# A mixture-of-experts trunk in float32: more slots in the ring of streamed weights, one buffer for the gathered tokens, and a slot that is handed back earlier

## The chip, the cores and the metric

The kernel runs on one core of a Trainium2 chip. The metric is the device time of one execution in microseconds; the median of three runs is compared. Engines are called as the profile calls them: PE (TensorE, with its weight loads as PEld), DVE (VectorE), ACT (ScalarE), POOL (GpSimd) and SP (SyncE, which only issues transfers here).

## The reference

Two decoder layers work on 256 positions of width 1024. Each layer has a mixer, a layer norm, a feed-forward part and a second layer norm. The feed-forward part of the first layer is one dense SwiGLU of width 2816. That of the second layer is a mixture of eight SwiGLU experts of width 3584, of which each position uses two:

```python
def swiglu(x, w_gate, w_up, w_down):
    return (jax.nn.silu(x @ w_gate) * (x @ w_up)) @ w_down

def moe_swiglu(x, w_router, e_gate, e_up, e_down):
    t = x.reshape(B * S, D)
    logits = (t @ w_router).astype(jnp.float32)
    top_val, top_idx = lax.top_k(logits, TOP_K)
    top_w = jax.nn.softmax(top_val, axis=-1)
    gates = jnp.sum(jax.nn.one_hot(top_idx, N_EXPERTS) * top_w[..., None], axis=1)
    out = jnp.zeros_like(t)
    for e in range(N_EXPERTS):
        out = out + gates[:, e:e + 1] * swiglu(t, e_gate[e], e_up[e], e_down[e])
    return out
```

All weights are float32, and all eight experts' weights (352 MB of the 426 MB that the kernel reads) pass through the core once.

## The kernel before

**Weights.** They stream in units of 128 x 2048 values (1 MB, 8 KB in each partition). A product needs two parts of each unit that the PE can multiply at its fast float32 rate: `h`, a rounded copy that ACT makes, and `l`, the rest that DVE makes by a subtraction (`split`, L270 to L272; only the first unit of each gate product, `whole`, is multiplied raw). A unit so passes through one slot as `r` (raw), and then through two others as `h` and `l`.

**Slots.** There are `NS` = 16 slots in the pool `wt` and `NX` = 2 more in the pool `more`, which takes the place of the pool `mix` once the mixer of the second layer no longer needs that. The class `Stream` keeps the order of all units (`plan`, with a due time for each, counted in ticks) and the list `idle` of slots that may be taken, first in, first out. `load` takes one slot and issues a transfer on SP. `converting` takes two, for `h` and `l`, and puts the raw slot at the end of the list. `drop` puts the slot of an `l` back, `free` what is left of the oldest unit. A slot is put back where the code issues the last instruction that uses it; who takes it next waits on the chip for that instruction.

**Order.** `manual_schedule` leaves each engine's instructions in the order of the code. A tick is one step of a product: one matmul with `h` and one with `l`. At each tick the pending tasks step first, and then `pump` runs: it loads while the list is longer than `1 + max(0, freed + reserve - split)`, then converts the next unit if it is due within `lead` = 12 ticks and the list has at least two slots.

**Experts.** An expert has four groups of columns: 512, 1024, 1024 and 1024 (in the last expert in reverse). For each group come the gate product, the up product, and then the down product of the group before. A product of 1024 columns has four units of four ticks, one of 512 columns two. After an up product, `finish` copies it out of PSUM, and 13 ticks later `transposed` folds and transposes the group's hidden values and splits them into `ch` and `cl` (rings of four), by way of a tile `hid`. After a whole expert, `scatter` adds its output rows to `acc`.

**Tokens.** An expert works on the tokens that were routed to it. `gather` picks them on the PE with a one-hot matrix: the transposes L1012, a copy `pt` by ACT, two times 16 matmuls L1000, and their split into `xh` and `xl` by `parts`; `xw` is a raw copy of the first half for the unsplit units. With at most 64 tokens (`few`) the parts `h` and `l` of the tokens lie side by side in one 128 wide operand, so that two passes do; with more (`many`, a wide expert) it takes three passes. Tokens have two buffers in turn (`xh`, `xl` in the pool `act`, rings of two): the gather for expert e + 1 is started after the third group's down product of expert e and runs four ticks later, in the fourth group's gate product.

**The lines of the steps below.** `h` is L271, `l` is L272, and L1050 is a pass over an unsplit unit. L1053 and L1060 are passes of gate and up products, L1137 and L1144 those of down products, L1032 the last passes of a pair of units. L1075 and L1085 are the copies out of a gate and an up product, L1108 the fold, and L1110 to L1113 the hidden values; L991, L992 and L1025 write the gathered tokens.

Of the kernel before, what the change touches and what calls it, by code (L numbers as in the profile page):

```python
# [8 lines left out]
F32 = mybir.dt.float32  # L9
# [18 lines left out]
TAU = 16.0  # L28

NS = 16  # L30
NX = 2
NR = 6
NQ = 3
NC = 5
# [5 lines left out]
def trunk(ctx: ExitStack, tc: tile.TileContext, x, w_in, gm_ws, gm_bs, gm_ln_g, gm_ln_b, gla_wa2, gla_ba,  # L40
# [24 lines left out]
        return mix.tile(list(shape), F32, tag="m2", name=name, bufs=5)  # L65

    def tiny(name, n, dt=F32):
        return act.tile([P, n], dt, tag="tiny", name=name, bufs=10, padded_shape=[P, 32])

    def psy(name, shape=(P, 512), dt=F32):  # L70
        return ps_y.tile(list(shape), dt, tag="y", name=name)
# [220 lines left out]
    def norm(y, st, gt, bt, nm):  # L292
# [5 lines left out]
        for hf in range(2):  # L298
            s = slice(hf * 512, hf * 512 + 512)
            nc.vector.scalar_tensor_tensor(y[:, s], y[:, s], mv[:, 0:1], gt[hf], op0=ALU.subtract, op1=ALU.mult)  # L300
            nc.vector.scalar_tensor_tensor(y[:, s], y[:, s], rs, bt[hf], op0=ALU.mult, op1=ALU.add)

    def to_T(tb, nm, xT):

        xh = act.tile([P, KT, P], F32R, tag="xh", name=f"xh{nm}{tb}")
        xl = act.tile([P, KT, P], F32R, tag="xl", name=f"xl{nm}{tb}")
        xT[tb] = xh, xl
        for hf in range(2):
            tp = psw(f"tp{nm}{tb}{hf}", (P, 4, P))
            for j in range(4):  # L310
                c = (hf * 4 + j) * P
                nc.tensor.transpose(tp[:, j, :], xf[tb][:, c:c + P], ident)
            split(xh[:, hf * 4:hf * 4 + 4, :], xl[:, hf * 4:hf * 4 + 4, :], tp)
            if hf == 0:
                yield 1
# [62 lines left out]
    def transposed_parts(sg, nm, kt):  # L378

        tp = psw(f"th{nm}", (P, 4, P))  # L380
        for j in range(kt):
            nc.tensor.transpose(tp[:, j, :], sg[:, j * P:(j + 1) * P], ident)
        ch = act.tile([P, 4, P], F32R, tag="ch", name=f"ch{nm}", bufs=4)
        cl = act.tile([P, 4, P], F32R, tag="cl", name=f"cl{nm}", bufs=4)
        split(ch[:, 0:kt, :], cl[:, 0:kt, :], tp[:, 0:kt, :])
        return ch, cl

# [84 lines left out]
    def mixer(l, xT, small, ready, nxT):  # L472
# [207 lines left out]
        products([("gv", l), ("gu", l)], xT, 512, f"gm{l}", gated)  # L680
        W.lead = 12
        products([("og", l)], xT, 512, f"og{l}", out_gate)
        if l == DEPTH - 1:

            mix_only.close()
            more = ctx.enter_context(tc.tile_pool(name="more", bufs=1))
            room.extend([more] * NX)
            idle.extend(range(NS, NS + NX))
        gb = load_gb(ln_mix_g[l], ln_mix_b[l], f"mix{l}")
        py = [[psy(f"wo{l}{tb}{hf}") for hf in range(2)] for tb in range(2)]  # L690

# [134 lines left out]

    def moe(xT, ready, consts):
        iota, pri, ones, ecst, pair, fold, powers = consts
        lg = const.tile([P, 2, NE], F32, name="lg")
        plt = psy("plt", (P, 2, NE))  # L830

# [29 lines left out]
        cnt_i = const.tile([P, 1], I32, name="cnt_i")  # L861
        mask_i = const.tile([P, 1], I32, name="mask_i")
        small = const.tile([P, NE], F32, name="small")
        acc = [room[-1].tile([P, D], F32, name=f"acc{tb}") for tb in range(2)]

        def routing():
            yield 2
# [83 lines left out]
        class Expert:  # L951
# [21 lines left out]

            def one_hot(self):
                nm = self.nm
                self.oh = act.tile([P, 2, P], F32, tag="oh", name=f"oh{nm}", bufs=1)
                self.twice = self.oh
                for tb in range(2):
                    nc.vector.tensor_scalar(self.oh[:, tb, :], iota, self.rank(tb), None, op0=ALU.is_equal)
                if self.fewer is not None:  # L980
                    self.twice = s2(f"oh2{nm}", F32, (P, 2, P))
                    slot = s2(f"slot{nm}")[:, 0:P]
                    nc.vector.tensor_scalar(slot, iota, HALF - 0.5, self.fewer, op0=ALU.is_ge, op1=ALU.mult)
                    nc.vector.tensor_tensor(slot, slot, iota, op=ALU.add)
                    for tb in range(2):
                        nc.vector.tensor_scalar(self.twice[:, tb, :], slot, self.rank(tb), None, op0=ALU.is_equal)
# [21 lines left out]
            def gather(self):  # L1008
                nm = self.nm
                tp = pst(f"oht{nm}", (P, 2, P))  # L1010
                for tb in range(2):
                    nc.tensor.transpose(tp[:, tb, :], self.twice[:, tb, :], ident)  # L1012
                self.pt = act.tile([P, 2, P], F32R, tag="pt", name=f"pt{nm}")
                nc.scalar.activation(self.pt, tp, AF.Copy)
                xh = act.tile([P, KT, P], F32R, tag="xh", name=f"exh{nm}")
                xl = act.tile([P, KT, P], F32R, tag="xl", name=f"exl{nm}")
                self.x = xh, xl
                for hf in range(2):
                    p = pst(f"gx{nm}{hf}", (P, 4, P))
                    self.pick(p, [xf[tb][:, hf * 512:hf * 512 + 512] for tb in range(2)])  # L1020
                    self.parts(xh[:, hf * 4:hf * 4 + 4, :], xl[:, hf * 4:hf * 4 + 4, :], p)
                    if hf == 0:
                        if self.wide is not None:
                            self.xw = room[-1].tile([P, 4, P], F32, tag="xw", name=f"xw{nm}", bufs=2)
                            nc.scalar.activation(self.xw, p, AF.Copy)  # L1025
                        yield 2

# [7 lines left out]
            def product(self, units, n, nm):  # L1035

                xh, xl = self.x
                nb = n // 512
                p = [psw(f"{nm}{b}") for b in range(nb)]
                kk = 2048 // n  # L1040
                held, rest, last = [], [], []
                for u, ((wh, wl), free, drop) in enumerate(units):
                    held.append(free)
                    for j in range(kk):
                        k = kk * u + j
                        for b in range(nb):
                            s = slice(b * 512, b * 512 + 512)
                            tick()
                            if wl is None:
                                nc.tensor.matmul(p[b], self.xw[:, k, :], wh[:, j, s], start=k == 0, stop=False,  # L1050
                                                 skip_group_check=True)
                                continue
                            nc.tensor.matmul(p[b], xh[:, k, :], wh[:, j, s], start=k == 0, stop=False,  # L1053
                                             skip_group_check=True)
                            rest.append((p[b], xl[:, k, :], wh[:, j, s], False))
                            second = p[b], xh[:, k, :], wl[:, j, s], k == KT - 1
                            if k == KT - 1 or (u % 2, j, b) == (1, kk - 1, nb - 1):
                                last.append(second)
                            else:
                                nc.tensor.matmul(*second[0:3], start=False, stop=False, skip_group_check=True)  # L1060
                    if u % 2 == 0:
                        drop()
                    if u % 2 and (nb > 1 or u == 1):
                        self.last_passes(rest, last)
                        for free in held:
                            free()
                        held, rest, last = [], [], []
                return p
# [28 lines left out]
            def transposed(self, nm, sg, up):  # L1097

                tp = pst(f"th{nm}", (P, 4, P))
                ch = act.tile([P, 4, P], F32R, tag="ch", name=f"ch{nm}", bufs=4)  # L1100
                cl = act.tile([P, 4, P], F32R, tag="cl", name=f"cl{nm}", bufs=4)
                hid = room[-1].tile([P, 4, HALF], F32, tag="hid", name=f"hid{nm}", bufs=2)

                def few():

# [47 lines left out]
            def scatter(self):  # L1153
                yp = []
                for hf in range(2):
                    yh = act.tile([P, 512], F32R, tag="ch", name=f"yh{self.nm}{hf}", bufs=4)
                    yl = act.tile([P, 512], F32R, tag="cl", name=f"yl{self.nm}{hf}", bufs=4)
                    split(yh, yl, self.y[hf])
                    yp.append((yh, yl))
                yield 3  # L1160
# [33 lines left out]
        products([("eg", 0, 0), ("eu", 0, 0)], xT, 512, "e0", first_done, ready)  # L1194
        while W.hold:
            tasks["route"].step()
        W.lead, W.reserve = LEAD_E, NC
        for i, t in enumerate((ybanks, ybanks, tbanks, tbanks)):
            t.append(psy(f"bank{i}"))

        def first_hidden():
            yield 4
            p = pst("gh", (P, 4, P))
            experts[0].pick(p, first, hidden_columns)
            ch = act.tile([P, 4, P], F32R, tag="ch", name="che0f", bufs=4)
            cl = act.tile([P, 4, P], F32R, tag="cl", name="cle0f", bufs=4)
            experts[0].parts(ch, cl, p)
            experts[0].hT[0] = [(ch, cl)]

# [5 lines left out]
        for e, ex in enumerate(experts):  # L1215
            for g, (c0, n) in enumerate(groups(e)):
# [10 lines left out]
                if last:  # L1227
                    W.cap = W.index[up_units(e, g)[-1]] + 2
                pu = ex.product(stream(up_units(e, g)), n, f"eu{e}{g}")
                task = Task(ex.finish(g, sg, pu, 3 if last else 13))  # L1230
                W.cap = len(W.plan) - 2 if last else len(W.plan)
                if prev in hidden_tasks:
                    hidden_tasks[prev].finish()
# [3 lines left out]
                prev = e, g  # L1237
                hidden_tasks[e, g] = task
                if g == NG - 2 and e + 1 < NE:
                    tasks["gather", e + 1] = Task(experts[e + 1].gather_from_scratch())  # L1240
        gb, y, sq = [W.slot(nm, F32, 2, D)[0] for nm in ("gb", "y", "sq")]
        for i, v in enumerate((ln_ffn_g[1], ln_ffn_b[1])):
            nc.sync.dma_start(gb[:, i, :], bcast(v, D))
# [157 lines left out]
```

## Time and profile before

| | before |
|---|---|
| three runs | 1342.61, 1344.07, 1343.92 us; median 1343.92 |
| the profiled execution | 1342.48 us, of which the span of its instructions is 1340.8 |
| PE, PEld, DVE, ACT busy | 1296.5, 1024.0, 1068.5, 839.0 us |
| moved by transfers | 426.35 MB, 318 GB/s over the span |

The expert weights are worked on from about 430 us to the end. A busy time is the union of an engine's instructions; those of the PE are pipelined, and their ends are modelled, so its share looks higher than its work is.

### The profile page before, as it was taken

How to read it: one execution, taken by the hardware profiler on the slowest of the kernel's cores; microseconds unless marked ns; L12 is line 12 of the kernel's file. 1: busy time of each engine (PE TensorE's matmuls, PEld its weight loads, DVE VectorE, ACT ScalarE, POOL GpSimd, SP SyncE). 2: the span in 40 equal slices, each digit the busy share in tenths (PEclk: the TensorE clock that was granted, in tenths of full speed). 3: DMA queues.
4: the chain of work that ended last, by engine and by line, in shares of the span. 5: the costliest groups of instructions: out<-in, count | busy, mean ns of one | idle time of the engine just before them, and what ended most of it. 6: DMA issues, size and time to landing. Idle time of an engine off the chain costs nothing. (4 is left out here: it accounts for less than half of the span.)

```text
span 1340.8 us, 16964 instructions
## 1 busy us (share of the span) xinstructions
PE 1296.5 (97%) x6113; PEld 1024.0 (76%) x6113; DVE 1068.5 (80%) x965; ACT 839.0 (63%) x702; POOL 37.7 (3%) x79
## 2 busy tenths in 40 slices
PE   8999999999998999999999999999999999999996
PEld 7878888888887788777778877776776776777774
DVE  6687544476684887898888789899899989989997
ACT  5653444346342666687756667776777777877783
POOL 1012000000110000000000000000000000000000
PEclk9999999999999999999999999999999999999998
DMA  9636656543484598999999899999999999999993
GB/s 343 256 126 205 240 188 204 203 157 132 159 301 162 222 365 321 392 370 380 408 368 369 320 384 370 389 408 412 408 389 408 409 393 410 407 400 403 412 407 118
DMA packets 118766, 426.35 MB, mean 318 GB/s; under 512 B 8089, under 2 KB 10722, under 8 KB 104578
## 3 DMA queue, kind: packets, MB, share of 16 engines
q1 hardware_dynamic: 117218, 420.61, 81.0%
q0 software_dynamic: 1440, 4.33, 1.1%
q8 instruction: 64, 1.05, 0.3%
q14 instruction: 44, 0.36, 0.1%
HBM read 423.86 MB, written 1.05 MB: 317 GB/s over the span
## 5 line engine op out<-in xcount | busy, mean ns | idle before, releaser
L272 DVE TENSOR_TENSOR l<-r,h 128x2048 fp32r<-128x2048 f32 (+2 forms) x373 | 833.3, 2249 | 134.0 <-ACT h L271 117.6
L271 ACT ACTIVATE h<-r 128x2048 fp32r<-128x2048 f32 (+2 forms) x373 | 685.0, 1881 | 124.1 <-PE bank L1032 39.1
L1137 PE MATMUL bank<-h,che 128*128 128x512 f32 x440 | 174.4, 396 | 0.0
L1053 PE MATMUL eu<-h,exh 128*128 128x512 f32 x440 | 167.5, 389 | 0.0
L1144 PE MATMUL bank<-l,che 128*128 128x512 f32 x377 | 153.3, 407 | 7.0 <-DVEq L969 3.5
L1060 PE MATMUL eu<-l,exh 128*128 128x512 f32 x361 | 141.0, 391 | 0.3 <-DVE l L272 0.3
L1053 PE MATMUL eg<-h,exh 128*128 128x512 f32 x316 | 128.2, 418 | 0.0
L1050 PE MATMUL eg<-r,xw 128*128 128x512 f32 x248 | 114.5, 595 | 0.0
L1144 PEld LDWEIGHTS bank<-l,che 128*128 128x128 f32 x377 | 70.8, 188 | 41.9 <-DVE l L272 17.1
L1053 PEld LDWEIGHTS eu<-h,exh 128*128 128x128 f32 x440 | 82.6, 188 | 16.9
L1137 PEld LDWEIGHTS bank<-h,che 128*128 128x128 f32 x440 | 82.8, 188 | 15.2
L1060 PE MATMUL eg<-l,exh 128*128 128x512 f32 x237 | 92.7, 391 | 0.1
L1060 PEld LDWEIGHTS eu<-l,exh 128*128 128x128 f32 x361 | 67.8, 188 | 15.9 <-DVE l L272 2.1
L1050 PEld LDWEIGHTS eg<-r,xw 128*128 128x128 f32 x248 | 45.2, 190 | 39.6 <-issue 37.8
L266 PE MATMUL f<-h,xhm 128*128 128x512 f32 (+1 forms) x192 | 72.2, 376 | 0.0
L267 PE MATMUL f<-l,xhm 128*128 128x512 f32 (+1 forms) x192 | 71.4, 372 | 0.0
L268 PE MATMUL f<-h,xlm 128*128 128x512 f32 (+1 forms) x192 | 71.4, 372 | 0.0
L1053 PEld LDWEIGHTS eg<-h,exh 128*128 128x128 f32 x316 | 59.5, 188 | 15.4 <-issue 4.1
L1110 ACT ACTIVATE hide<-bank 128x256 f32<-128x256 f32 x42 | 16.1, 384 | 71.7 <-PE bank L1108 71.7
L1060 PEld LDWEIGHTS eg<-l,exh 128*128 128x128 f32 x237 | 44.6, 188 | 12.7 <-issue 3.8
L1075 ACT ACTIVATE sge<-eg 128x512 f32<-128x512 f32 x55 | 30.2, 595 | 36.4 <-PE eg L1032 36.3
L1108 PEld LDWEIGHTS bank<-fold,sge 128*128 128x128 f32 x336 | 46.0, 196 | 5.2 <-issue 2.4
(354 smaller groups left out, 1803.3 us busy)
## 6 DMA issues: line engine op xcount, KB each, us to landing
r<-in_exp_w_gate SPq DMA_DIRECT2D x112, 1024.0 KB, 11.1
r<-in_exp_w_up SPq DMA_DIRECT2D x112, 1024.0 KB, 7.5
r<-in_exp_w_down SPq DMA_DIRECT2D x110, 1024.0 KB, 11.6
r<-in_w_in SPq DMA_DIRECT2D x17, 1024.0 KB, 8.5
r<-in_ffn_w_gate SPq DMA_DIRECT2D x11, 1024.0 KB, 6.9
r<-in_ffn_w_up SPq DMA_DIRECT2D x11, 1024.0 KB, 5.3
r<-in_ffn_w_down SPq DMA_DIRECT2D x11, 1024.0 KB, 4.9
r<-in_w_out SPq DMA_DIRECT2D x8, 1024.0 KB, 9.2
```

Of the source, the lines that this page charges most:

```text
L266: nc.tensor.matmul(ps, xh, wh, start=start, stop=False)
L267: nc.tensor.matmul(ps, xh, wl, start=False, stop=False)
L268: nc.tensor.matmul(ps, xl, wh, start=False, stop=stop)
L271: nc.scalar.activation(dst_h, src, AF.Copy)
L272: nc.vector.tensor_tensor(dst_l, src, dst_h.bitcast(F32), op=ALU.subtract)
L1050: nc.tensor.matmul(p[b], self.xw[:, k, :], wh[:, j, s], start=k == 0, stop=False, skip_group_check=True)
L1053: nc.tensor.matmul(p[b], xh[:, k, :], wh[:, j, s], start=k == 0, stop=False, skip_group_check=True)
L1060: nc.tensor.matmul(*second[0:3], start=False, stop=False, skip_group_check=True)
L1075: nc.scalar.activation(o, i, f)
L1108: nc.tensor.matmul(tp[:, j, i * HALF:i * HALF + HALF], hidden_columns(t, j), fold, start=True, stop=True)
L1137: nc.tensor.matmul(y, ch[:, k, :], wh[:, j, s], start=first and u + j == 0, stop=False, skip_group_check=True)
L1144: nc.tensor.matmul(y, ch[:, k, :], wl[:, j, s], start=False, stop=False, skip_group_check=True)
```

## The change

`NX` goes from 2 to 4, and one more slot, number `NS + NX`, is added to the pool `wt`: 21 slots instead of 18 while the experts run. What makes room for them:

- The tokens have one buffer (`x_parts`). While the layers are dense, the second block of 128 positions uses the new slot (`slot_parts`), which joins the list once the first expert products are through. The next expert's gather is started behind the last up product of an expert instead of within its last gate product, and `one_hot` alone stays where it was.
- `ch` and `cl` of the experts are rings of two, those of the dense part lie in the pool `mix`. `hid` lies in the gate copy that it is made from; `oh`, `slot`, `yh` and `yl` join the ring `s2` of six; `xw` has one buffer, and `tiny` a ring of 7.
- `mix` is closed at the start of `moe` and no longer in the second mixer.
- In `product` an unsplit unit is freed as soon as its own passes are issued, and no longer together with the unit after it. The last group's hidden values are made 9 ticks after its up product instead of 3.

```diff
-NX = 2
+NX = 4
...
-        return act.tile([P, n], dt, tag="tiny", name=name, bufs=10, padded_shape=[P, 32])
+        return act.tile([P, n], dt, tag="tiny", name=name, bufs=7, padded_shape=[P, 32])
...
+    def x_parts(nm):
+
+        return [act.tile([P, KT, P], F32R, tag=f"x{i}", name=f"x{i}{nm}", bufs=1) for i in "hl"]
+
+    def slot_parts(nm):
+
+        t = wt.tile([P, 2048], F32R, tag=f"w{NS + NX}", name=f"x{nm}").rearrange("p (i k n) -> p i k n", i=2, k=KT)
+        return t[:, 0], t[:, 1]
...
-        xh = act.tile([P, KT, P], F32R, tag="xh", name=f"xh{nm}{tb}")
-        xl = act.tile([P, KT, P], F32R, tag="xl", name=f"xl{nm}{tb}")
+        xh, xl = x_parts(f"{nm}{tb}") if tb == 0 else slot_parts(f"{nm}{tb}")
...
-        ch = act.tile([P, 4, P], F32R, tag="ch", name=f"ch{nm}", bufs=4)
-        cl = act.tile([P, 4, P], F32R, tag="cl", name=f"cl{nm}", bufs=4)
+        ch = mix.tile([P, 4, P], F32R, tag="ch", name=f"ch{nm}", bufs=4)
+        cl = mix.tile([P, 4, P], F32R, tag="cl", name=f"cl{nm}", bufs=4)
...
-        if l == DEPTH - 1:
-
-            mix_only.close()
-            more = ctx.enter_context(tc.tile_pool(name="more", bufs=1))
-            room.extend([more] * NX)
-            idle.extend(range(NS, NS + NX))
...
     def moe(xT, ready, consts):
         iota, pri, ones, ecst, pair, fold, powers = consts
+
+        mix_only.close()
+        more = ctx.enter_context(tc.tile_pool(name="more", bufs=1))
+        room.extend([more] * NX + [wt])
+        idle.extend(range(NS, NS + NX))
...
+        def hidden_parts(nm):
+            return [more.tile([P, 4, P], F32R, tag=t, name=f"{t}{nm}", bufs=2) for t in ("ch", "cl")]
...
-                self.oh = act.tile([P, 2, P], F32, tag="oh", name=f"oh{nm}", bufs=1)
+                if self.fewer is not None:
+                    slot = s2(f"slot{nm}")[:, 0:P]
+                self.oh = s2(f"oh{nm}", F32, (P, 2, P))
...
-                xh = act.tile([P, KT, P], F32R, tag="xh", name=f"exh{nm}")
-                xl = act.tile([P, KT, P], F32R, tag="xl", name=f"exl{nm}")
-                self.x = xh, xl
+                self.x = xh, xl = x_parts(f"e{nm}")
...
-                            self.xw = room[-1].tile([P, 4, P], F32, tag="xw", name=f"xw{nm}", bufs=2)
+                            self.xw = more.tile([P, 4, P], F32, tag="xw", name=f"xw{nm}", bufs=1)
...
                 for u, ((wh, wl), free, drop) in enumerate(units):
-                    held.append(free)
+                    if wl is not None:
+                        held.append(free)
...
-                    if u % 2 == 0:
+                    if wl is None:
+                        free()
+                    elif u % 2 == 0:
                         drop()
...
-                ch = act.tile([P, 4, P], F32R, tag="ch", name=f"ch{nm}", bufs=4)
-                cl = act.tile([P, 4, P], F32R, tag="cl", name=f"cl{nm}", bufs=4)
-                hid = room[-1].tile([P, 4, HALF], F32, tag="hid", name=f"hid{nm}", bufs=2)
+                ch, cl = hidden_parts(nm)
+                hid = sg[:, 0:4 * HALF].rearrange("p (a b) -> p a b", a=4)
...
-                    yh = act.tile([P, 512], F32R, tag="ch", name=f"yh{self.nm}{hf}", bufs=4)
-                    yl = act.tile([P, 512], F32R, tag="cl", name=f"yl{self.nm}{hf}", bufs=4)
+                    yh = s2(f"yh{self.nm}{hf}", F32R)
+                    yl = s2(f"yl{self.nm}{hf}", F32R)
...
         while W.hold:
             tasks["route"].step()
+        idle.append(NS + NX)
         W.lead, W.reserve = LEAD_E, NC
...
-                task = Task(ex.finish(g, sg, pu, 3 if last else 13))
+                task = Task(ex.finish(g, sg, pu, 9 if last else 13))
+                if g == NG - 1 and e + 1 < NE:
+
+                    tasks["gather", e + 1] = Task(experts[e + 1].gather())
...
                 if g == NG - 2 and e + 1 < NE:
-                    tasks["gather", e + 1] = Task(experts[e + 1].gather_from_scratch())
+                    experts[e + 1].one_hot()
```

## Rows read from the trace of the kernel before

**Rows 1.** The page: the span, the busy time of each engine, the transfers' busy share in 40 slices (tenths) and what they moved.

```profile
span 1340.8 us, 16964 instructions
...
PE 1296.5 (97%) x6113; PEld 1024.0 (76%) x6113; DVE 1068.5 (80%) x965; ACT 839.0 (63%) x702; POOL 37.7 (3%) x79
...
DMA  9636656543484598999999899999999999999993
GB/s 343 256 126 205 240 188 204 203 157 132 159 301 162 222 365 321 392 370 380 408 368 369 320 384 370 389 408 412 408 389 408 409 393 410 407 400 403 412 407 118
```

**Rows 2.** Busy time of each engine in stretches of the span: length, then PE, PEld, DVE, ACT and POOL in us with their instructions, the granted clock, the transfers' share and GB/s.

```profile
680.00:820.00 140.00, 138.70 (x616) 109.68 (x615) 112.91 (x73) 92.65 (x69) 0.00 (x0) 1.00 0.91 352
820.00:1300.00 480.00, 463.74 (x2166) 355.81 (x2165) 440.41 (x319) 362.70 (x288) 0.00 (x0) 1.00 1.01 404
1300.00:1341.00 41.00, 27.99 (x125) 20.24 (x123) 31.58 (x44) 18.88 (x23) 1.96 (x2) 0.90 0.44 170
```

**Rows 3.** The costliest groups of instructions from 820 to 1300 us: busy time, mean ns of one, idle time of the engine before them and what ended it.

```profile
L272 DVE TENSOR_TENSOR l<-r,h 128x2048 fp32r<-128x2048 f32 x170 | 386.0, 2289 | 33.4 <-ACT h L271 23.1 <-DVEq L969 3.3 <-PE bank L1032 0.5
L271 ACT ACTIVATE h<-r 128x2048 fp32r<-128x2048 f32 x170 | 315.6, 1913 | 24.5 <-PE bank L1032 9.4 <-PE eg L1032 7.9 <-PE eg L1050 7.2
```

**Rows 4.** What ACT waited for from 460 to 1300 us: total, times, the longest.

```profile
ACT hide L1110 <- PE bank L1108: 70.9, 38, 3.4
ACT h L271 <- PE bank L1032: 39.1, 24, 4.2
...
ACT h L271 <- PE eg L1050: 9.4, 7, 1.8
...
ACT xw L1025 <- DVE exh L992: 2.9, 6, 0.5
...
ACT xw L1025 <- DVE exl L272: 0.8, 1, 0.8
```

**Rows 5.** DVE in order of time around the gather for expert 6 (start, length, and in brackets the idle time before, with what ended it).

```profile
1074.53 2.28 DVE L272 TENSOR_TENSOR l<-r,h 128x2048 fp32r<-128x2048 f32 x1
1077.23 0.42 DVE L992 TENSOR_TENSOR exh<-bank,exh 128x256 fp32r<-128x256 f32 x1 [0.42 <-ACT exh L991]
1080.12 2.29 DVE L272 TENSOR_TENSOR l<-r,h 128x2048 fp32r<-128x2048 f32 x1 [2.46 <-ACT h L271]
...
1087.69 9.26 DVE L272 TENSOR_TENSOR l<-r,h 128x2048 fp32r<-128x2048 f32 x4 [0.36 <-ACT h L271]
...
1106.69 4.68 DVE L272 TENSOR_TENSOR l<-r,h 128x2048 fp32r<-128x2048 f32 x2 [0.27 <-ACT h L271]
1112.24 4.68 DVE L272 TENSOR_TENSOR l<-r,h 128x2048 fp32r<-128x2048 f32 x2 [0.87 <-ACT h L271]
```

**Rows 6.** ACT in order of time in the same stretch.

```profile
1076.82 0.38 ACT L991 ACTIVATE exh<-bank 128x256 fp32r<-128x256 f32 x1 [2.27 <-DVE l L272]
1077.69 0.60 ACT L1025 ACTIVATE xw<-bank 128x512 f32<-128x512 f32 x1 [0.49 <-DVE exh L992]
1078.18 1.90 ACT L271 ACTIVATE h<-r 128x2048 fp32r<-128x2048 f32 x1
...
1092.95 1.08 ACT L1085 ACTIVATE upe<-eu 128x512 f32<-128x512 f32 x2
...
1109.80 0.60 ACT L1075 ACTIVATE sge<-eg 128x512 f32<-128x512 f32 x1 [1.34 <-PE eg L1032]
1110.30 3.71 ACT L271 ACTIVATE h<-r 128x2048 fp32r<-128x2048 f32 x2
```

**Rows 7.** PE in order of time in the same stretch: the gate product of the last group of expert 5 (L1050 on), the gather (L1012, L1000), the first pass of the up product and the first of the down product after it.

```profile
1071.11 2.79 PE L1050 MATMUL eg<-r,xw 128*128 128x512 f32 x6
1073.74 0.38 PE L1012 MATMUL bank<-ident,oh 128*128 128x128 f32 x2
1074.76 2.02 PE L1000 MATMUL bank<-oh,xin 128*128 128x128 f32 x16 [0.63 <-DVE che L1113]
...
1077.93 1.95 PE L1000 MATMUL bank<-oh,xin 128*128 128x128 f32 x16
...
1084.73 0.39 PE L1053 MATMUL eu<-h,exh 128*128 128x512 f32 x1
...
1091.98 0.39 PE L1137 MATMUL bank<-h,che 128*128 128x512 f32 x1
```

**Rows 8.** ACT, and then DVE, in the dense feed-forward part of the first layer, in order of time.

```profile
167.12 1.92 ACT L271 ACTIVATE h<-r 128x2048 fp32r<-128x2048 f32 x1 [2.36 <-DVE l L272]
...
164.79 2.29 DVE L272 TENSOR_TENSOR l<-r,h 128x2048 fp32r<-128x2048 f32 x1 [1.78 <-ACT h L271]
169.07 2.29 DVE L272 TENSOR_TENSOR l<-r,h 128x2048 fp32r<-128x2048 f32 x1 [1.98 <-ACT h L271]
```

**Rows 9.** DVE in the second group of expert 6 (first row), ACT and DVE in its third group (the next four), and DVE in the first group of expert 7 (last row).

```profile
1138.96 4.68 DVE L272 TENSOR_TENSOR l<-r,h 128x2048 fp32r<-128x2048 f32 x2 [0.88 <-ACT h L271]
...
1156.79 0.39 ACT L1110 ACTIVATE hide<-bank 128x256 f32<-128x256 f32 x1 [3.34 <-PE bank L1108]
1157.07 3.71 ACT L271 ACTIVATE h<-r 128x2048 fp32r<-128x2048 f32 x2
...
1146.21 9.26 DVE L272 TENSOR_TENSOR l<-r,h 128x2048 fp32r<-128x2048 f32 x4 [0.37 <-ACT h L271]
...
1215.78 9.26 DVE L272 TENSOR_TENSOR l<-r,h 128x2048 fp32r<-128x2048 f32 x4 [0.27 <-ACT h L271]
```

More of the change, by code (lines that the diff above doesn't have):

```diff
@@ L863, in moe @@
         small = const.tile([P, NE], F32, name="small")
-        acc = [room[-1].tile([P, D], F32, name=f"acc{tb}") for tb in range(2)]
+        acc = [more.tile([P, D], F32, name=f"acc{tb}") for tb in range(2)]
+        def hidden_parts(nm):
+            return [more.tile([P, 4, P], F32R, tag=t, name=f"{t}{nm}", bufs=2) for t in ("ch", "cl")]
         def routing():
@@ L981, in one_hot @@
                     self.twice = s2(f"oh2{nm}", F32, (P, 2, P))
-                    slot = s2(f"slot{nm}")[:, 0:P]
                     nc.vector.tensor_scalar(slot, iota, HALF - 0.5, self.fewer, op0=ALU.is_ge, op1=ALU.mult)
@@ L1204, in first_hidden @@
             experts[0].pick(p, first, hidden_columns)
-            ch = act.tile([P, 4, P], F32R, tag="ch", name="che0f", bufs=4)
-            cl = act.tile([P, 4, P], F32R, tag="cl", name="cle0f", bufs=4)
+            ch, cl = hidden_parts("e0f")
             experts[0].parts(ch, cl, p)
```

## The prediction

> **What bounds the kernel now.** The page comes first [rows 1]: PE is busy 97% of the span, DVE 80%, and the transfers' share is at its top in the last third. Busy shares are a mean over stages, so the stretches follow [rows 2]. From 680 to 820 us, where expert 2 needs three passes, PE is busy 138.7 of 140 us while DVE has 27 us and the transfers 9% to spare: a PE stage. From 820 to 1300 us, the experts with two passes, three things are nearly full at once: PE by its modelled ends, DVE with 440 of 480 us, and the transfers with a share of 1.01 at 404 GB/s. The question is which of them is late. ACT turns each landed unit into `h` and would be the first to notice a late transfer. Its waits from 460 to 1300 us [rows 4] name PE and DVE; no row of that view, shown or left out, names a transfer. So the data lies there when it is wanted, and the pace is that of the loop DVE makes `l`, PE uses it, PE gives slots back, ACT and DVE make the next. In that loop DVE is idle 33.4 us before its `l`, 23.1 of them because ACT's `h` is late [rows 3]. The reader is to see that a microsecond is won here only if DVE's idle time shrinks.
>
> **The three slots.** Following `pump` through the code: it keeps loading while the list is longer than its bound, so a slot more is a unit more that lies raw. Converting still starts at most 12 ticks ahead. Raw units in hand grow from 8 to 10 to 11 to 13, and nothing else. A unit takes 1.05 MB at 404 GB/s = 2.6 us [rows 2], so transfers can run up to 7.8 us further ahead in the PE stages, where they have idle time. As ACT waits for none, I take 0 of it; the other end is -7.8 us.
> The same gap recurs in DVE at each gather and elsewhere, 23.1 us in all [rows 3]. If it came from a lack of slots, three more would take it away; but the extra ones go to raw units before an `h` can have them, so I take 0 here too. The Trainium skill (Perfetto Trace Analysis, Optimization Strategy) speaks the other way: the same gap repeating on the engine that should be full can mean that there isn't enough SBUF for the next tile. By that rule the sum below would hold -23.1 us in place of 0.
>
> **The unsplit unit freed at once.** This looks like the smallest edit, and I think it decides. Take a group of 1024 columns. At tick 4 of the gate product the first up unit is converted; that empties the list, and its raw slot goes to the end. Before, the list then held one slot until tick 8, too few to convert. At tick 8 the unsplit unit and the second gate unit gave back three; the list of four passed the bound of three, a load took the raw slot, and the second up unit's `h` got the unsplit unit's slot, which PE had long finished with. After the change the unsplit unit's slot arrives four ticks early. At tick 8 the list holds the raw slot of the first up unit and that slot: two, enough to convert, and not over the bound, which the early `free` has raised to two. So the second up unit's `h` takes the slot in which the first one still lies raw, and ACT must wait until DVE has finished the first one's `l`. Then DVE has no `h` to work on. In a group of 512 columns the same falls on the second down unit. That is one hit in each of the 31 groups that have an unsplit unit.
> The dense part shows what a hit costs [rows 8]: ACT waits 2.36 us for DVE, and DVE is then idle 1.98. There PE was the bound and it cost nothing. The bounds are thus 0 from below, and from above 1.98 for each of the 23 groups outside the wide experts 0 and 2 and the very last group (by then all weights are loaded and the list is long): 45.5 us. The value between them comes from one turn, expert 5 to 6, group by group:
> - Fourth group, second up unit: with the gather gone from this place nothing else fills DVE, 2.0 us.
> - First group of the next expert: `h` started at 1110.30 [rows 6] and now has to wait for an `l` that ended at 1106.69 + 4.68 = 1111.37 [rows 5], so +1.1 us.
> - Second group: what the wait adds (under 1 us, as the two `acc` sums stand between) falls into a gap of 0.88 that comes two units later [rows 9]: 0.
> - Third group: `h` comes at 1157.07 in any case, behind the copy `hide`, and the `l` before it ended by 1146.21 + 9.26 = 1155.47 [rows 9]: 0.
>
> **The gather moved.** Before, it cost DVE 0.42 + 2.46 = 2.88 us [rows 5]: ACT waited for the picks, then `xw` waited for DVE's `exh` as it does time after time, seven times in all [rows 4], and only then came the next `h`. Behind the up product the picks are done while ACT still copies that product out, 1.08 us [rows 6], but `exh` now stands behind queued `l`, and `xw` (0.60) and the next `h` (1.90) still lie between two steps of DVE: 2.5 us plus the handover, say 2.6. Gain 0.3. Queued behind that wait are the `h` for the last down unit and the gate units of the next expert.
> On PE 4.1 us of transposes and picks leave the gate product, which lasted 13.62 us, from 1071.11 to 1084.73 [rows 7], and come between up and down product. 32 passes of the up product take 7.25 us there [rows 7], 0.227 each, so the gate product without the gather ends about 4 us earlier; PE then stalls 1.5 + 0.4 + 0.6 us in the up product for the late `l` of the first hit, does the gather, and finds the down units ready but the last. That catching up of DVE while PE gathers is worth 0.6. PE's wait of 0.63 for a bank goes too, inside this.
> So a turn costs 2.0 + 1.1 - 0.3 - 0.6 = 2.2 us.
>
> **The rest, at nothing.** With `mix` closed later the second mixer's end has 16 slots as the first layer's had; no ACT wait on a transfer follows. The new slot for the second block of tokens stands where the second buffer stood. The rings of two: the first block's `ch` is rewritten at tick 13 of a down product whose first eight ticks read it, and the last group's 9 ticks keep that order; without it PE would stand for a fold, about 2 us a group. In `s2` each tile's last reader comes at least one product before the sixth allocation after it. `hid` in the gate copy is written after the folds that read this. A ring of 7 for `tiny` holds two gate norms. The number of instructions stays.
>
> **The sum.** Turns 3 to 4, 4 to 5 and 5 to 6: 3 x 2.2 = 6.6. Turn 6 to 7 without the first-group hit, as expert 7 starts with 1024 columns: 1.1. Turn 1 to 2 runs into a PE stage: 0.5. Expert 7: DVE works through four `l` without a gap [rows 9] and gets one of 2.0 in its first and one in its third group: 4.0; the second group again absorbs. Wide experts: 0. Together +12.2 us on the profiled execution's 1342.5 = 1354.7. That execution lies 1.4 us below the median of the runs, so I say 1355. The end itself, the last stretch there, moves along [rows 2].
>
> **Rivals.**
> *The transfers bind after all (faster).* For it: share 1.01 over 480 us [rows 2]. Against: no wait of ACT names a transfer [rows 4]. It would give 1344 - 7.8 = 1336. It decides if ACT waits for landings in the last expert, where transfers and conversion come closest. 7%.
> *The gather's move pays, and the hits are covered (faster).* If PE's 4.1 us at the new place give DVE time for the hit and `xw` no longer waits, a turn gains up to 2.9; over the five gathers into experts 2 and 4 to 7 that is up to 14 us, and half of it more likely: 1337. It needs the picks done before DVE reaches `exh`. 8%.
> *The slots do relieve `h` (faster).* 1344 - 23 = 1321; against it stands the order of the list. 4%. It is what the rule of the Trainium skill cited above (Perfetto Trace Analysis, Optimization Strategy) would bring.
> *No change.* The hits fall where ACT is late anyway, as in the second and third groups, and DVE's idle time only changes place: 1342 to 1347. 11%.
> *The forecast (slower)*, from +3 us to +25, the latter when the hits of second and first groups and of turn 1 to 2 add in full (23 at 1.1). 70% with what lies above it.
>
> **How the numbers follow.** Three runs lie within 0.11% of each other, so 0.2% (2.7 us) is about what can be told from no change. Faster 0.19, same 0.11, slower 0.70, as the cases above add up. The range reaches down to the first two rivals, 1336, and up to 1344 + 25 = 1369. Within slower alone it is 1347 to 1369.
>
> **What would show it.** In the changed profile ACT's `h` waits for DVE's `l` some 20 to 30 times from 460 to 1300 us, over 30 us in total, where before there is no such row [rows 4]; DVE's wait for `h` from 820 to 1300 grows from 23.1 to 30 to 40 us [rows 3]; the gather stands between the last up product and the down product, still with `xw` behind `exh`; transfers in the PE stages have a higher share, and the loads' landings lie further ahead of their use. If the waits of `h` on `l` are there and the time is the same, the covering was misjudged; if they are not there, the list was misread; if the time falls by 7 us with no change in DVE's gaps, the transfers did bind.

## The result, and the profile after

The changed kernel takes 1356.51 us (median of four runs, 1355.47 to 1357.44), against 1343.26 for the kernel before beside it: a ratio of 1.0098, interval 1.0081 to 1.0116. It is slower by 13.3 us; 1355 was forecast, with a range of 1336 to 1369. Its profiled execution took 1357.34, of which the span is 1355.6.

First the page of the changed kernel: span, busy times, and the transfers' share and rate in 40 slices.

```profile
span 1355.6 us, 16946 instructions
...
PE 1304.7 (96%) x6113; PEld 1024.2 (76%) x6113; DVE 1068.1 (79%) x965; ACT 835.8 (62%) x702; POOL 36.7 (3%) x79
...
DMA  9636655544467799799999989999999999999981
GB/s 346 246 127 210 236 190 204 186 155 156 147 225 279 271 361 377 298 401 408 387 372 361 354 321 379 408 391 395 404 395 385 412 405 379 407 412 390 383 351 65
```

DVE does the same work as before, 1068.1 us against 1068.5 [rows 1]; its share is lower only because the span is longer. So the loss is idle time. Its place is seen in the stretches (columns as in rows 2):

```profile
680.00:820.00 140.00, 138.34 (x611) 108.94 (x610) 111.55 (x74) 90.09 (x66) 0.00 (x0) 1.00 0.89 346
820.00:1300.00 480.00, 459.46 (x2126) 348.98 (x2125) 430.86 (x315) 352.49 (x283) 0.00 (x0) 1.00 1.00 398
1300.00:1356.00 56.00, 41.82 (x186) 30.28 (x184) 45.76 (x50) 31.89 (x33) 1.96 (x2) 0.91 0.43 166
```

From 820 to 1300 us DVE has 9.6 us less work done, and the transfers bring 398 GB/s in place of 404 [rows 2]. The costliest groups of that stretch name the cause of DVE's idle time:

```profile
L272 DVE TENSOR_TENSOR l<-r,h 128x2048 fp32r<-128x2048 f32 x166 | 377.0, 2290 | 45.2 <-ACT h L271 34.6 <-DVEq L980 2.2 <-DMA r<-in_exp_w_gate 2.0
L271 ACT ACTIVATE h<-r 128x2048 fp32r<-128x2048 f32 x166 | 307.9, 1911 | 65.6 <-DVE l L272 61.3 <-PE bank L1042 4.3
```

DVE waits 34.6 us for `h`, 23.1 before [rows 3]. ACT's `h` in turn waits 61.3 us for DVE's `l`, which ended none of its waits there before. The view of ACT's waits from 460 to 1300 us (total, times, longest) counts them:

```profile
ACT h L271 <- DVE l L272: 99.2, 29, 5.7
ACT sge L1122 <- PE bank L1120: 45.7, 24, 3.4
ACT h L271 <- PE bank L1042: 22.2, 14, 4.3
ACT xw L1035 <- DVE xhe L1004: 13.7, 6, 3.2
```

29 hits, where [rows 4] has none; the wait of `xw` for the gathered tokens is there too, and longer than the 2.9 us of before. (`sge` at L1122 is the old `hide`, which now lies in the gate copy.) One turn from expert 5 to expert 6 shows two hits and the gather. DVE, in order of time, as rows 5, with the third group of expert 7 as its last row:

```profile
1082.64 4.67 DVE L272 TENSOR_TENSOR l<-r,h 128x2048 fp32r<-128x2048 f32 x2
1089.29 13.84 DVE L272 TENSOR_TENSOR l<-r,h 128x2048 fp32r<-128x2048 f32 x6 [1.98 <-ACT h L271]
1103.47 0.42 DVE L1004 TENSOR_TENSOR xhe<-bank,xhe 128x256 fp32r<-128x256 f32 x1 [0.34 <-DVEq L980]
1106.36 2.29 DVE L272 TENSOR_TENSOR l<-r,h 128x2048 fp32r<-128x2048 f32 x1 [2.47 <-ACT h L271]
...
1122.47 4.57 DVE L272 TENSOR_TENSOR l<-r,h 128x2048 fp32r<-128x2048 f32 x2 [1.99 <-ACT h L271]
...
1296.19 4.50 DVE L272 TENSOR_TENSOR l<-r,h 128x2048 fp32r<-128x2048 f32 x2 [1.98 <-ACT h L271]
```

ACT in the same turn:

```profile
1087.34 3.72 ACT L271 ACTIVATE h<-r 128x2048 fp32r<-128x2048 f32 x2 [3.94 <-DVE l L272]
...
1103.93 0.60 ACT L1035 ACTIVATE xw<-bank 128x512 f32<-128x512 f32 x1 [3.18 <-DVE xhe L1004]
...
1120.52 1.92 ACT L271 ACTIVATE h<-r 128x2048 fp32r<-128x2048 f32 x1 [3.29 <-DVE l L272]
```

And PE there, in the up product of the last group and at the gather behind it:

```profile
1091.63 0.50 PE L1071 MATMUL eu<-l,xhe 128*128 128x512 f32 x1 [1.23 <-DVE l L272]
...
1097.92 0.38 PE L1024 MATMUL bank<-ident,oh 128*128 128x128 f32 x2
1098.14 1.95 PE L1012 MATMUL bank<-oh,xin 128*128 128x128 f32 x16
```

DVE ended two `l` at 1087.31. Only then could ACT start the next `h` (1087.34, after 3.94 us of waiting), and DVE stood still for 1.98 us until that `h` was done. PE met the missing `l` at 1091.63. The second hit, in expert 6's first group, leaves DVE idle for 1.99 us, where [rows 5] has 0.87: 1.1 more.

To see where the time goes, follow the end of the same unit's `l` through both traces:

| unit | before | after | later by |
|---|---|---|---|
| last gate of the second mixer | 344.7 | 345.7 | 1.0 |
| expert 0, 4th group, 2nd gate unit | 495.9 | 497.9 | 2.0 |
| expert 1, 3rd group, 4th gate unit | 587.8 | 591.2 | 3.4 |
| expert 2, 2nd group, 3rd gate unit | 670.4 | 674.3 | 3.9 |
| expert 3, 2nd group, 1st up unit | 804.5 | 810.1 | 5.6 |
| expert 4, 2nd group, 3rd gate unit | 905.5 | 912.7 | 7.2 |
| expert 5, 2nd group, 1st up unit | 1023.1 | 1031.6 | 8.5 |
| expert 6, 2nd group, 3rd gate unit | 1124.1 | 1134.2 | 10.1 |
| expert 7, 1st group, 4th gate unit | 1218.1 | 1229.1 | 11.1 |
| expert 7, 1st group, 1st down unit | 1262.3 | 1275.2 | 12.9 |
| expert 7, 2nd group, 2nd down unit | 1292.9 | 1307.6 | 14.7 |

### The profile page after: what moved, and what is told of

Same layout as the page of the kernel before. It is cut to its first block, busy times and chain, and to the rows that moved or that the text cites. A ratio compares the mean times of both kernels' runs of the same rounds, so it can differ in the third digit from the quotient of the medians.

```text
span 1355.6 us, 16946 instructions
## 1 busy us (share of the span) xinstructions
PE 1304.7 (96%) x6113; PEld 1024.2 (76%) x6113; DVE 1068.1 (79%) x965; ACT 835.8 (62%) x702; POOL 36.7 (3%) x79
## 5 line engine op out<-in xcount | busy, mean ns | idle before, releaser
L1064 PE MATMUL eu<-h,xhe 128*128 128x512 f32 x440 | 167.8, 390 | 0.0
L1071 PE MATMUL eu<-l,xhe 128*128 128x512 f32 x361 | 143.3, 397 | 9.4 <-DVE l L272 8.7
L1064 PE MATMUL eg<-h,xhe 128*128 128x512 f32 x316 | 127.6, 416 | 0.0
L1064 PEld LDWEIGHTS eu<-h,xhe 128*128 128x128 f32 x440 | 82.6, 188 | 16.9
L1071 PE MATMUL eg<-l,xhe 128*128 128x512 f32 x237 | 92.8, 392 | 0.0
L1071 PEld LDWEIGHTS eu<-l,xhe 128*128 128x128 f32 x361 | 67.7, 188 | 32.1 <-DVE l L272 18.3
L1064 PEld LDWEIGHTS eg<-h,xhe 128*128 128x128 f32 x316 | 59.4, 188 | 15.7 <-issue 4.1
L1071 PEld LDWEIGHTS eg<-l,xhe 128*128 128x128 f32 x237 | 44.6, 188 | 12.9 <-issue 2.6
L1122 ACT ACTIVATE sge<-bank 128x256 f32<-128x256 f32 x42 | 16.0, 381 | 50.2 <-PE bank L1120 46.5
L1120 PE MATMUL bank<-fold,upe 128*128 128x64 f32 x336 | 46.4, 281 | 0.0
L271 ACT ACTIVATE chf<-thf 128x512 fp32r<-128x512 f32 (+1 forms) x12 | 6.7, 560 | 61.3 <-PE thf L390 61.3
L1120 PE MATMUL bank<-fold,sge 128*128 128x64 f32 x336 | 43.8, 273 | 0.0
## 6 DMA issues: line engine op xcount, KB each, us to landing
r<-in_exp_w_gate SPq DMA_DIRECT2D x112, 1024.0 KB, 11.7
```

The costliest lines, as they stand in the source:

```text
L271: nc.scalar.activation(dst_h, src, AF.Copy)
L1120: nc.tensor.matmul(tp[:, j, i * HALF:i * HALF + HALF], hidden_columns(t, j), fold, start=True, stop=True)
L1122: nc.scalar.activation(hid, tp[:, :, 0:HALF], AF.Silu)
```

## Experiments

Three causes were put against each other at first: A, the slot that `h` takes after the early freeing; B, the gather's new place with one buffer; C, the slots themselves through their transfers. Later D: the recurring gap comes of too few slots. All times are medians; the kernel before stood at 1342.9 in the first two sets of four and at 1343.45 in the third.

**The early freeing alone, in the kernel before.**

```diff
-                    held.append(free)
+                    if wl is not None:
+                        held.append(free)
...
-                    if u % 2 == 0:
+                    if wl is None:
+                        free()
+                    elif u % 2 == 0:
                         drop()
```

> The kernel before, with the early freeing of the unsplit unit as its only change: 18 slots, two buffers of tokens, the gather in its old place. Theory A (the list of slots: ACT's h takes the slot in which the unit before it still lies raw, and waits for DVE's l): the waits of h on l appear here as they do in the changed kernel, 25 to 31 of them and 85 to 110 us in all from 460 to 1300 us, and the time rises by 10 to 20 us, 1353 to 1363. Theory B (the gather in its new place with one buffer and a longer wait of xw for DVE costs the time): no change, 1342 to 1345. Theory C (the three slots cost the time, by more transfers at the same time as the work): no change, 1342 to 1345.

Measured: 1355.58 (ratio 1.0091, 1.0076 to 1.0107). ACT's waits from 460 to 1300 us:

```profile
ACT h L271 <- DVE l L272: 85.8, 29, 5.4
```

The same 29 hits and a loss of 12.7 us, with 18 slots, two buffers and the gather in its old place. A holds; neither B nor C is needed for the loss.

**The changed kernel without the early freeing** (the same lines put back).

> The changed kernel without the early freeing: the unsplit unit is freed together with the unit after it, as before; 21 slots and the moved gather stay. Theory A: no wait of h on l from 460 to 1300 us, and the time of the kernel before less what the moved gather gives, 0.2 to 0.9 us in each of five turns: 1338 to 1344. Theories B and C: what costs the time is still there, 1354 to 1358.

Measured: 1338.48 (0.9963, 0.995 to 0.9977). The top of ACT's waits, and further down what is left of those of `h` on `l`:

```profile
ACT sge L1119 <- PE bank L1117: 62.5, 30, 3.4
ACT sge L1085 <- PE eg L1042: 38.0, 24, 3.4
...
ACT h L271 <- DVE l L272: 3.4, 2, 1.9
```

A said none; of 29 waits two are left, at 487 and 1294 us. Both also stand, to within 2 us, in the next run (with one more at 696), whose rule for the list allows no hit. Everything else that the change does gives 4.4 us; the early freeing on top of it costs 18.0 (1356.51 less 1338.48, measured in different sets).

**The early freeing kept, another slot for `h`.**

```diff
+            if idle[0] == self.last_raw:
+                idle[0:2] = idle[1], idle[0]
+            self.last_raw = slot
             h, sh = self.slot(f"h{i}", F32R, a, b)
             l, sl = self.slot(f"l{i}", F32R, a, b)
```

> The changed kernel with the early freeing kept. One thing is added: where the first slot of the list is the one in which the unit before still lies raw, h takes the second slot and l takes the first. Theory A: the l before it is done by then on the same engine, so nothing waits, and the time is that of the changed kernel without the early freeing within 2 us, 1338 to 1344. Theories B and C: 1354 to 1358. If it is the early freeing itself that costs the time and not the slot that h takes, this one stays at 1354 to 1358 while the one without the early freeing falls.

Measured: 1335.58 (0.9941, 0.9927 to 0.9954), 2.4 us under the range of A. The early freeing itself is harmless; what costs is which of two slots `h` takes. The rule only exchanges the two. By the medians this kernel is even 2.9 us faster than the one without the early freeing, but the executions of the two overlap, and the rule also takes away hits in the dense part, which the other still has.

**The gather alone moved, in the kernel before.**

```diff
+                if g == NG - 1 and e + 1 < NE:
+                    tasks["gather", e + 1] = Task(experts[e + 1].gather())
...
-                    tasks["gather", e + 1] = Task(experts[e + 1].gather_from_scratch())
+                    experts[e + 1].one_hot()
```

> The kernel before with the gather alone moved: its one-hot matrix is made where it was, and the gather starts behind the last up product of an expert. 18 slots, two buffers of tokens, no early freeing. Theory A: a gain of 0.2 to 0.9 us in each of five to seven turns, 1338 to 1343. Theory B: the loss appears here, 1350 to 1358. Theory C: no change, 1342 to 1345.

Measured: 1334.85 (0.9941, 0.9928 to 0.9955), a gain of 8.0, more than A allowed. B is wrong in sign. DVE in the turn from expert 5 to 6:

```profile
1068.81 18.42 DVE L272 TENSOR_TENSOR l<-r,h 128x2048 fp32r<-128x2048 f32 x8
1087.58 0.42 DVE L992 TENSOR_TENSOR exh<-bank,exh 128x256 fp32r<-128x256 f32 x1 [0.34 <-DVEq L969]
1090.47 2.29 DVE L272 TENSOR_TENSOR l<-r,h 128x2048 fp32r<-128x2048 f32 x1 [2.47 <-ACT h L271]
...
1104.82 4.67 DVE L272 TENSOR_TENSOR l<-r,h 128x2048 fp32r<-128x2048 f32 x2 [0.23 <-ACT h L271]
```

Eight `l` in a row without a gap, where [rows 5] has gaps of 0.42, 2.46 and 0.36 among them. The 2.47 at the gather itself is still there, as forecast. Its own two gaps fall from 2.88 to 2.81 together. What is won here are small gaps behind it: of 0.36, 0.27 and 0.87 in [rows 5], 0.23 is left.

**Two of the three slots taken away** (`NX = 2` in the changed kernel).

> The changed kernel with two of its three extra slots taken away: 19 slots in place of 21, all else as it is. Theory A says that the slots carry neither loss nor gain as long as no transfer is late, and that the order of the list alone decides: 31 waits of h on l as before, 1353 to 1359. Theory C (three more slots cost time through transfers that come at another time): half of the loss or more is gone, 1343 to 1350. Theory D (the slots give something that the early freeing hides): slower than the changed kernel, 1360 or more.

Measured: 1357.41 (1.0106, 1.009 to 1.0121), the changed kernel's time, with the same waits to the digit:

```profile
ACT h L271 <- DVE l L272: 99.2, 29, 5.7
```

C falls, and at this pace the slots carry nothing.

**Three small edits with 18 slots:** gather moved, early freeing, and the rule for `h`.

> The kernel before with 18 slots and two buffers of tokens, with three small edits: the gather moved, the unsplit unit freed at once, and h kept out of the slot in which the unit before still lies raw. Theory A: no wait of h on l, the gain of the moved gather alone (1334.85), and up to 3 us more, as the slot that comes back early lets units be converted sooner: 1331 to 1336. If the extra slots were needed for the 1335.6 of the 21 slots with the same list rule, this one is slower than that, 1337 or more.

Measured: 1333.13 (0.9921, 0.9907 to 0.9934), as A has it. 18 slots do as well as 21 did under that rule (1335.58, in a kernel with the change's other edits as well).

**The slots given to converted units.** The changed kernel with the rule, and then:

```diff
-NC = 5
+NC = 8
...
-LEAD_E = 12
+LEAD_E = 16
```

> The changed kernel with the rule that keeps h out of that slot, and the three slots given to converted units in place of raw ones: a reserve of 8 and not 5, and a lead of 16 ticks and not 12. Theory D (the recurring gap of DVE before l comes of too few slots for the next unit): DVE's wait for h from 460 to 1300 us falls from 65 us by a third or more, and the time by 5 to 10 us, to 1326 to 1331. Theory A: ACT's h is late because ACT stands behind a fold or the gather, not for a slot, and raw units fall to 7 or 8; the time stays within 3 us of 1335.6.

Measured: 1330.58 (0.99, 0.9885 to 0.9915). The `l` group from 460 to 1300 us, where the run with the rule alone had 65.5 for `ACT h`:

```profile
L276 DVE TENSOR_TENSOR l<-r,h 128x2048 fp32r<-128x2048 f32 x288 | 657.8, 2291 | 56.3 <-ACT h L275 37.6 <-DVEq L984 2.7 <-DVE l L276 0.9
```

As D has it: the gap shrinks by 43%, the time by 5.0.

**A reserve of 6,** lead as it was (`NC = 6`, with the rule).

> The changed kernel with the rule that keeps h out of that slot, and a reserve of 6 and not 5, so that a unit is always converted 12 ticks ahead (with 5 it was 11 in about a third of the cases); raw units fall from 12 to 10 on average. Theory D: half or less of the gain of the run with a reserve of 8, 1331 to 1335. Theory A: 1333 to 1337.

Measured: 1323.87 (0.9851, 0.9837 to 0.9864); again in the third set:

> The same kernel as the run with a reserve of 6 in 21 slots, on the same chip as the next three: 1322 to 1326.

Measured: 1322.93 (0.985, 0.9833 to 0.9866). I had expected it between the last two; it is the fastest of all, 20 us under the kernel before. With a reserve of 5 the list, followed through the code, was short of a slot in somewhat under half of the conversions, and these came 11 ticks ahead. One slot more, and a unit is always converted 12 ticks ahead. The gain over the run with the rule alone is 11.7, more than twice that of the run before, though DVE's wait for `h` falls less, from 65.5 to 44.9 where it fell to 37.6:

```profile
L276 DVE TENSOR_TENSOR l<-r,h 128x2048 fp32r<-128x2048 f32 x289 | 656.5, 2290 | 61.9 <-ACT h L275 44.9 <-DVEq L984 3.8 <-DMA r<-in_exp_w_down 1.8
```

So D has the sign but not the measure: the size of that gap alone does not give the time. The run before had a longer lead as well, and the last run below shows a longer lead costing time.

**The same with 18 slots** (the three small edits and `NC = 6`).

> The kernel with 18 slots and the three small edits (gather moved, unsplit unit freed at once, h kept out of the slot in which the unit before still lies raw), and a reserve of 6 and not 5, so that units are always converted 12 ticks ahead; 7 to 8 units lie raw instead of 10 to 11. If the three extra slots carry nothing even at the faster pace: 1322 to 1326, as with 21 slots. If raw units run out, ACT's h waits for landings in the last experts and the gain over 1333 is mostly lost: 1328 to 1335. I hold the second for the likelier, as landings came 0.1 to 4 us before their use in the last experts already with 21 slots and a reserve of 6.

Measured: 1328.07 (0.9884, 0.9867 to 0.99), 5.1 slower than with 21 on the same chip. ACT's waits from 820 to 1300 us:

```profile
ACT h L275 <- DMA r<-in_exp_w_gate: 13.9, 16, 2.5
...
ACT h L275 <- DMA r<-in_exp_w_up: 7.4, 12, 1.6
ACT h L275 <- DMA r<-in_exp_w_down: 5.9, 13, 0.6
```

With 21 slots:

```profile
ACT h L275 <- DMA r<-in_exp_w_gate: 4.4, 2, 2.5
...
ACT h L275 <- DMA r<-in_exp_w_up: 1.3, 2, 0.8
...
ACT h L275 <- DMA r<-in_exp_w_down: 0.5, 2, 0.2
```

27.2 us of waits for landings where the other has 6.2. Up to expert 4 the 18 slots are ahead, by 3.1 us at its second group (1.7 of them from before the experts); by expert 7's first down unit they are 5.3 behind. At this pace raw units run out, and here the change's slots pay. The two kernels differ in the change's other edits too; it is the waits for landings that speak for the slots.

**The hits multiplied** (`NC = 6` in the changed kernel, without the rule).

> The changed kernel with a reserve of 6 and not 5 as its only change; h may take the slot of the unit before again. By the order of the list that now happens 130 times and not 30. Theory A: each time h and l follow one another, 1.9 and 2.3 us, and no longer overlap, so the waits of h on l grow to 100 or more, 250 us or more in all, and the kernel is far slower than the changed one: 1380 to 1480. If a unit that is converted at once is worth more than the waits cost: 1324 to 1350.

Measured: 1545.46 (1.1509, 1.149 to 1.1528), beyond the range of A. ACT's waits from 460 to 1300 us (a smaller part of this span), then the stretch from 820 to 1300:

```profile
ACT h L271 <- DVE l L272: 260.8, 96, 7.8
```

```profile
820.00:1300.00 480.00, 404.73 (x1719) 305.54 (x1718) 345.88 (x252) 287.27 (x226) 0.00 (x0) 0.93 0.83 317
```

One slot of reserve is worth 11.7 us under the rule for `h` and costs 189 us without it (1545.46 less 1356.51).

**A lead of 14** (with the rule and `NC = 6`).

> As the run with a reserve of 6 in 21 slots with the rule for h, and a lead of 14 ticks and not 12. If the distance between conversion and use still sets the pace: 1316 to 1322. If the transfers set it now (share 1.02, landings 0.1 us before their use at the end): 1322 to 1328.

Measured: 1329.94 (0.9905, 0.9888 to 0.9921), slower than a lead of 12 by 7.0, and outside both expectations. Why is not known.

## Why the prediction was right, step by step

- **The hits: right in place, and in price once the gather is moved.** They make the loss, by the run with nothing else and by the two that take them away. A gap of 1.98 was forecast for each from the dense part [rows 8], and 1.98 to 1.99 is what DVE shows. In the fourth group PE was to stall some 2.5 us; it stands for 1.5 in two stalls, the first of them the 1.23 shown. Over the second and third groups the forecast was 0: ACT waits there too (5.7 and 2.1 us in expert 6), and the lag behind the kernel before is 10.1 us on either side of them. Between like kernels (the changed one and the one without early freeing) an expert's period, from one copy `pt` to the next, is 110.8 against 107.6 us: 3.2 for the hits of a turn, 2.0 + 1.1 = 3.1 forecast. With the gather in its old place the early freeing alone takes the period only from 109.2 to 111.0, 1.8.
- **The gather: right sign, too small.** A gain of 0.9 a turn was forecast. The period fell from 109.2 to 107.5 with the gather alone moved, 1.7; on top of the hits the rest of the change, with the moved gather, gives 0.2 (111.0 to 110.8). That the wait at `xw` would stay was right, but its own two gaps gave 0.07 and not 0.3. The term that was too small is the 0.6 for catching up: the small gaps behind the gather, 1.50 together in [rows 5], fell to 0.23. Gain and hits don't add, as the forecast took them to: the moved gather gives 8.0 without hits, the hits cost 12.7 with the gather in its old place, and their sum, 4.7, is far from 13.3. The reading that fits is that a hit's wait lies where the small gaps were, so that a gap can be won only once: in the same turn of the run with the early freeing alone, the 0.36 is gone behind the hit's 1.65, and the 0.87 has become 1.98.
- **Turns by turn.** From 3 to 4, 4 to 5 and 5 to 6 the table has 1.6, 1.3 and 1.6, together 4.5 where 6.6 stood: the gather again. From 1 to 2, 0.5 as said. From 6 to 7, 1.0 against 1.1. Expert 7, 3.6 against 4.0. Two lines were missed: "Wide experts: 0" left out that the turns out of experts 0 and 2 end in the first group of an expert with two passes; they cost 1.4 and 1.7. So the sum came out through errors of both signs, and that it lies within 1.1 us of the 13.3 measured is in part luck. (Added to the median of the runs and not to the profiled execution, +12.2 gives 1356.1; 1355 was said.)
- **2.0 us before expert 0 ends** stood nowhere in the sum. 1.0 of them is there at 345 us, where the profiled executions of this study scatter from -0.6 to +2.6 with like code there (+0.3 with two slots less); it is not shown to belong to the change.
- **The slots at 0: right here.** Two less change nothing. Landings moved ahead as forecast: in the last group of expert 7 the first up unit landed 10.3 us before its `h`, 0.3 before the change. But they did so as soon as the slots joined, not in the PE stages: those have a share of 0.89, no higher than [rows 2]. The reason given was too narrow, though. ACT waits for no transfer only as long as DVE's gaps hold the pace down; with these gone, 18 slots are 5.1 us slower than 21.
- **The rule of the Trainium skill** (Perfetto Trace Analysis, Optimization Strategy), that a gap repeating on the engine that should be full can mean too little SBUF for the next tile, would have had the change gain 23 us. The trace disagrees for this change: the gap grew from 23.1 to 34.6 us, and what it grew by came from the order in which slots were taken. It agrees in part for the runs that let converted units have a slot more (11.7 us).
- **What stays open.** The changed kernel without early freeing is 3.6 us slower than the kernel before with the gather alone moved (1338.48, 1334.85). In their profiled executions, 4.7 apart, 2.2 of that stand at 345 us already, where it may be scatter, and 4.2 by expert 3; the period from there on is the same (107.6, 107.5). One of the untested edits (rings of two, `hid` in the gate copy, the later closing of `mix`, nine ticks at the end) may cost it; each was put at nothing, and none was tried alone.

## What to carry to other kernels

A buffer is free for the program as soon as its last use is issued, and for the chip when that use is done: from a first-in, first-out list, handing one back earlier can put a buffer that is still being read ahead of one that has long been idle. So when the time of a release changes, write out who takes each slot and what its last reader is, and look in the waits for two engines that release each other; give the earlier buffer to the output of the engine that reads it last. Extra buffers pay only once such waits are gone, and then in the place that is short: here one slot for a converted unit was worth 11.7 us, and three for raw units 0, and about 5 afterwards.

## What the runs showed of the hardware

The granted clock fell with PE's idle time. In the run with the hits multiplied PE was busy for 404.73 of 480 us from 820 to 1300, and the clock was 0.93 in the mean; in the changed kernel it was busy for 459.46, and the clock was 1.00. Within the first: from 910 to 920 us PE was busy for 5.62 us, and from 920 to 930, when it was busy throughout, the clock was 0.69 in the mean. So some of that run's PE work was done at a lower clock. Whether and how much this adds to the 189 us was not measured.
